# HGRN2 chunk products as eight levels of one form, dilated scores with both row halves in one step

## The chip, the cores and the metric

The kernel runs on one core of one Trainium2 chip. The metric is the device time of one execution in microseconds (us); the median of three runs of the kernel before is 2509.81 us (2506.52 to 2512.93). A core has a matmul engine (TensorE, PE in the profile; its weight loads are PEld), a vector engine (DVE), a scalar engine (ACT), a GpSimd engine (POOL) and a sync engine (SP) that here only issues DMAs. Each works through its own instructions in order; they wait for each other by semaphores. SBUF is the core's working memory with 128 partitions, PSUM the memory that PE writes, in eight banks of 128 x 512 f32.

## The reference

Two layers of a decoder trunk: 512 tokens, width 1024, f32. Each layer has a parallel token mixer of four branches (A dilated sliding-window attention in three groups, B differential attention, C HGRN2, D RWKV-7), gates, a merge, a cross-attention and a gated MLP with a convolution. The change touches C and A. C works in chunks of 64 tokens (4 heads of width 64); for one chunk it computes

```python
b = jnp.cumsum(lfc, axis=2)
diff = b[:, :, :, None, :] - b[:, :, None, :, :]
decay = jnp.exp(jnp.where(causal, diff, -jnp.inf))
att = jnp.einsum('bhtk,bhtsk,bhsk->bhts', qc, decay, kc)
o = o_inter + jnp.einsum('bhts,bhsv->bhtv', att, ic)
```

so that each product of query t and key s carries a decay for each of 64 channels. In A, each of three groups has 4 heads of width 64; a query of a block of 128 sees its own block and, in the first group, the one before:

```python
s = jnp.einsum('brhnqd,brhnkd->brhnqk', qb, kb).astype(F32) * dh ** -0.5
m = jnp.max(s, axis=-1, keepdims=True)
p = jnp.exp(s - m)
```

## The kernel before

**Two kinds of PE work.** The projections are dense: 128x128 weights against 512 tokens, each as three fp32r products of high and low parts (mm3 and ws_run, L405 on). A weight chunk `wst` comes by DMA, ACT casts the high part `whi` (L482), DVE subtracts for the low part `wlo` (L483), and the products gather in one of four PSUM banks (tag `pd`, L422). The branches' own products are small f32 matmuls, of which each is two MATMUL instructions in the trace; they use the other four banks (tag `ps`, L425).

**The order of the work** is set in Python by a planner (Weave, L294). It has one queue of dense work and a number of chains, which are generators. When a chain says `yield v`, its next step falls due at the planner's PE time plus v times a scale (0.856, for the chains `At` 1.84 times that, `csc`); until then dense work is put on PE. PE time is counted by rule (Tensor.matmul, L281: n/600 us for an f32 matmul of n columns), not measured. The tile framework then orders the instructions of each engine and adds the waits.

**Branch C** (branch_c, chain `Cb`) runs on PE while projection D (`Dp`) is the dense work. `b` is the running sum of the log decays. The chunk products are split by dyadic levels: level(h) (L816) makes X, which holds q times exp(b - b_mid) in the later h tokens of each block of 2h and k times exp(b_mid - b) in the earlier h; a product of X with itself is right in the upper right h x h corner of each block, and the mask U{h} takes just that corner. DVE subtracts (L823), ACT takes two exps, POOL makes two products (L826, L827). Levels 16, 8, 4 and 2 (L868 on) take for each row half p (two heads live in partitions 0 to 63, two in 64 to 127) and each pair of token blocks u one bank, four matmuls of 64 rows x 128, then a copy_predicated on DVE (L879) into `catt`. Levels 64 and 32 are there in a form of their own: narrow products for just the corners (L855 on), 64x64 and 32x32, with ACT copies. The diagonal and its neighbour (s = t and s = t - 1) are sums over channels: POOL and DVE make the products `cpr` (L804 to L810), PE sums them by a matrix of two columns, `hsel` (L836 on), ACT copies the sums to `csm`, and DVE spreads them over an identity (L852, L853).

**Dp's evacuation** shares the engines: DVE takes each finished bank to `Dp_draw` (L1030), POOL makes the difference of neighbouring tokens `Dp_ddd` (L1031), DVE mixes them into `dr`, `dk`, ... (L1034).

**Branch A** (attn_a, chain `At`) goes through banks of scores: a_scores puts the products of one row half p into one bank, DVE masks and takes the maxima, ACT the exps; a_turn transposes on PE and copies on ACT; a_out multiplies by v. With two halves there are 8 banks in the first group and 4 in each of the others, and the steps of neighbouring banks overlap. b_scores, in branch B, already takes the two row halves in turn, each into its own bank, and so do the products of D (`Db_ps<-dfar,dfbk`).

**rstd** (L576) sums squares over partitions by matmuls with two columns of ones. With `perm=True` (the chain `r1`, L1940) it also does so for the tokens at stride 4, into four more columns that no line reads except to copy them (L747).

Of the kernel before, what the change touches and what calls it, by code (L numbers as in the profile page):

```python
# [372 lines left out]
class Trunk:  # L373
# [1680 lines left out]
```

## Time and profile before

| | |
|---|---|
| median of three runs | 2509.81 us |
| the profiled execution, its own time | 2507.58 us |
| its span from first to last instruction | 2505.8 us |
| PE busy | 2456.6 us (98%), 13360 instructions |
| DVE busy | 1538.8 us (61%) |
| ACT busy | 996.3 us (40%) |
| POOL busy | 498.4 us (20%) |

The profile is of one execution. PE works nearly all the time, the other engines much less; what PE waits for is short in sum. The matmuls are pipelined, so the busy time of one says little about its cost: the distance between the starts of two neighbours does. A dense matmul of 128x512 starts every 0.227 us at the full granted clock (1.00 in the windows, 2.4 GHz) and every 0.427 us at 0.50 (1.2 GHz).

### The profile page before, as it was taken

Reading aid. Unit: us, or ns where it says so; the run is one execution under the profiler, and the core shown is the slowest. Engines: PE = TensorE matmul, PEld = TensorE weight load, DVE = VectorE, ACT = ScalarE, POOL = GpSimd, SP = SyncE. Lnnn points to the kernel's source line nnn. Section 1 sums busy time; section 2 is a strip of 40 time slices with the busy share of each in tenths; the row PEclk is TensorE's granted clock in tenths of the full one; section 3 lists DMA queues with packets and bytes.
Section 4 is the critical chain, followed back from the end, with each engine's and each line's share of the span. In section 5 each row is a group of like instructions: output and inputs, shape, how many; then the busy total and the mean of one; then the engine's idle time right before and its main releaser. Section 6 shows DMA issues by size and latency. Waiting matters only on the chain.

```text
span 2505.8 us, 34400 instructions
## 1 busy us (share of the span) xinstructions
PE 2456.6 (98%) x13360; PEld 2036.9 (81%) x13360; DVE 1538.8 (61%) x2751; ACT 996.3 (40%) x1769; POOL 498.4 (20%) x382
## 2 busy tenths in 40 slices
PE   8999999999999999999999999999999999999997
PEld 7777888778889888888897788877888898888886
DVE  7678356855655667366466773577556565762763
ACT  6332423434344444234362325244343344441441
POOL 1421033234010111001123110423330101110112
PEclk9899999999999999999999999999999999999998
DMA  4224334223423222322321242332234241222321
GB/s 171 82 87 145 98 116 145 67 66 126 143 97 132 88 93 93 101 93 101 127 88 52 92 146 95 121 119 77 67 123 143 98 152 60 92 101 93 101 93 59
DMA packets 89602, 259.62 MB, mean 104 GB/s; under 512 B 18144, under 2 KB 21856, under 8 KB 89440
## 3 DMA queue, kind: packets, MB, share of 16 engines
q1 hardware_dynamic: 57168, 205.81, 24.7%
q10 hardware_dynamic: 25872, 30.52, 3.7%
q0 software_dynamic: 6400, 21.11, 2.6%
q8 instruction: 105, 1.72, 0.3%
q14 instruction: 57, 0.47, 0.1%
HBM read 234.26 MB, written 23.13 MB: 103 GB/s over the span
## 4 chain that ended last, share of the span: by engine, by line
PE 92%; DVE 5%; ACT 1%; issue 1%; DMA 1%; POOL 0%; DVEq 0%; ACTq 0%; SPq 0%; POOLq 0%
PE ffn_pd L287 29%; PE A_pd L287 7%; PE Bp_pd L287 5%; PE Dp_pd L287 4%; PE Cp_pd L287 4%; PE ga_pd L287 3%; PE mo_pd L287 3%; PE mq_pd L287 3%; PE mix_pd L287 3%; PE gd_pd L287 3%; PE gc_pd L287 3%; PE Db_ps L287 3%; PE Cb_ps L287 3%; PE At_ps L287 2%; PE mk_pd L287 2%; PE mv_pd L287 2%
## 5 line engine op out<-in xcount | busy, mean ns | idle before, releaser
L482 ACT CAST whi<-wst 128x1024 fp32r<-128x1024 f32 x388 | 406.0, 1051 | 743.5 <-PE ffn_pd L287 216.1
L483 DVE TENSOR_TENSOR wlo<-wst,whi 128x1024 fp32r<-128x1024 f32 x388 | 494.1, 1277 | 212.3 <-ACT whi L482 211.0
L287 PE MATMUL ffn_pd<-xgh,whi 128*128 128x512 f32 x704 | 274.3, 390 | 0.0
L287 PE MATMUL ffn_pd<-xgh,wlo 128*128 128x512 f32 x704 | 273.9, 389 | 0.0
L287 PE MATMUL ffn_pd<-xgl,whi 128*128 128x512 f32 x704 | 273.9, 389 | 0.0
L1918 POOL TENSOR_TENSOR ffn_ft<-ffn_ft,ffn_fc 128x512 f32<-128x512 f32 x44 | 60.2, 1368 | 545.6 <-DVE ffn_fu L1904 350.3
L287 PEld LDWEIGHTS ffn_pd<-xgl,whi 128*128 128x128 f32 x704 | 132.1, 188 | 27.5
L287 PEld LDWEIGHTS ffn_pd<-xgh,wlo 128*128 128x128 f32 x704 | 132.1, 188 | 27.5
L287 PEld LDWEIGHTS ffn_pd<-xgh,whi 128*128 128x128 f32 x704 | 132.2, 188 | 27.2
L287 PE MATMUL ffn_pd<-fh,whi 128*128 128x512 f32 x352 | 136.9, 389 | 0.0
L287 PE MATMUL ffn_pd<-fl,whi 128*128 128x512 f32 x352 | 136.9, 389 | 0.0
L287 PE MATMUL ffn_pd<-fh,wlo 128*128 128x512 f32 x352 | 136.9, 389 | 0.0
L287 PE MATMUL A_pd<-xgh,whi 128*128 128x512 f32 x256 | 107.1, 418 | 0.0
L287 PE MATMUL A_pd<-xgh,wlo 128*128 128x512 f32 x256 | 100.9, 394 | 0.0
L287 PE MATMUL A_pd<-xgl,whi 128*128 128x512 f32 x256 | 100.5, 393 | 0.0
L1905 DVE TENSOR_TENSOR ffn_fu<-ffn_pd,r_rbc 128x512 f32<-128x512 f32 x88 | 60.4, 688 | 43.8 <-PE ffn_pd L287 43.5
L1468 POOL TENSOR_TENSOR A_rp<-A_rp,snr 128x512 f32<-128x512 f32 x24 | 52.1, 2172 | 174.4 <-DVE A_rp L1467 174.4
L530 DVE TENSOR_TENSOR fl<-ffn_ft,fh 128x512 fp32r<-128x512 f32 x44 | 30.5, 692 | 90.6 <-ACT fh L529 90.6
L529 ACT CAST fh<-ffn_ft 128x512 fp32r<-128x512 f32 x44 | 27.3, 621 | 144.8 <-POOL ffn_ft L1918 144.8
L574 POOL TENSOR_TENSOR mo_sqa<-mo_sqa,mo_sqt 128x512 f32<-128x512 f32 x14 | 23.6, 1684 | 297.8 <-ACT mo_sqa L570 257.9
L1907 ACT ACTIVATE ffn_fc<-ffn_fu,cvt 128x512 f32<-128x512 f32 x88 | 71.7, 817 | 26.8 <-DVE ffn_fu L1905 26.6
L287 PEld LDWEIGHTS ffn_pd<-fl,whi 128*128 128x128 f32 x352 | 66.1, 188 | 13.8
(601 smaller groups left out, 6342.8 us busy)
## 6 DMA issues: line engine op xcount, KB each, us to landing
wst<-in_wst_dram SPq DMA_DIRECT2D x388, 512.0 KB, 3.5
gb_gate<-gb_gu ACTq DMA_DIRECT2D x16, 256.0 KB, 2.2
gd_gate<-gd_gu ACTq DMA_DIRECT2D x16, 256.0 KB, 2.1
gc_gate<-gc_gu ACTq DMA_DIRECT2D x16, 256.0 KB, 2.0
pc_gu<-gc_gate POOLq DMA_DIRECT2D x16, 256.0 KB, 3.9
pd_gu<-gd_gate POOLq DMA_DIRECT2D x16, 256.0 KB, 3.0
pb_gu<-gb_gate POOLq DMA_DIRECT2D x16, 256.0 KB, 3.5
x<-in_x_dram ACTq DMA_DIRECT2D x13, 256.0 KB, 3.8
```

Source lines behind the costliest of these rows:

```text
L287: return self.te.matmul(out, lhsT, rhs, **kw)
L482: nc.scalar.copy(hi, st)
L483: nc.vector.tensor_sub(lo, st, hi.bitcast(F32))
L529: nc.scalar.copy(dst[0], src)
L530: nc.vector.tensor_sub(dst[1], src, dst[0].bitcast(F32))
L574: (eng or nc.gpsimd).tensor_add(acc[:, :n], acc[:, :n], t[:, :n])
L1468: nc.gpsimd.tensor_mul(t2, t2, self.snr)
L1905: nc.vector.tensor_mul(u[:, 2:514], ps, self.rb)
L1907: nc.scalar.activation(acc, u[:, 2:514], AF.Identity, scale=self.cv('cw2', ch), bias=self.cv('cb', ch))
L1918: nc.gpsimd.tensor_mul(th, th, cc[1])
```

## The change

In C the sums by `hsel` and the narrow form are gone. There are eight levels of one form: 0 (the diagonal: k against q themselves), 1 (made by first(): exp of one step's decay times q in odd tokens, a copy of k in even ones), 64, 32, 16, 8, 4, 2. The four `catt` tiles are set to zero on POOL at the start. A level is one step: for each u two banks, and the four products of the row halves p = 0 and p = 1 in turn, 16 matmuls of 64 rows x 128 in four banks. Levels 64 and 32 are copied by ACT, the others by DVE's copy_predicated (there is a new mask U0). In A, a step takes both row halves: their scores in turn into two banks, then the transposes of both, then the outputs of all four heads in one bank. The first group has 4 steps instead of 8, the others 2 instead of 4, with longer yields. r1 no longer makes the permuted sums. The diff, cut to its core:

```diff
-for _h in (1, 2, 4, 8, 16, 32):
+for _h in (0, 1, 2, 4, 8, 16, 32):
...
+    u[:, UM['U0']:UM['U0'] + 128] = p == f
...
-            if perm:
-                self.te.matmul(ps[:, 2 * (nt + t):2 * (nt + t) + 2], acc[:, t:512:4], self.ones[:, 0:2],
-                                 start=True, stop=True)
+        nw = nt
...
-        pr = [ar.alloc([P, 2, 512], name='cpr') for _ in range(2)]
         od = lambda x, o: x.rearrange("p j (n a) -> p j n a", a=2)[:, :, :, o]
-        nc.gpsimd.tensor_mul(pr[0], q, k)
-        nc.scalar.activation(od(pr[1], 0), od(lf, 1), AF.Exp)
-        nc.vector.tensor_mul(od(pr[1], 0), od(pr[1], 0), od(q, 1))
-        nc.vector.tensor_mul(od(pr[1], 0), od(pr[1], 0), od(k, 0))
-        nc.gpsimd.memset(od(pr[1], 1), 0.0)
-        ar.free(lf)
...
-        X64, X64t = level(64)
-        X32, X32t = level(32)
-        yield 4
-        att = [[None, None], [None, None]]
+        def first():
+
+            X = ar.alloc([P, 2, 512], name='cX')
+            nc.scalar.activation(od(X, 1), od(lf, 1), AF.Exp)
+            nc.gpsimd.tensor_mul(od(X, 1), od(X, 1), od(q, 1))
+            nc.gpsimd.tensor_copy(od(X, 0), od(k, 0))
+            ar.free(lf)
+            return X, X
...
         mm = self.te.matmul
-        ps = self.pss()
-        for x in range(2):
-            for t in range(NT):
-                for j in range(2):
-                    o = 16 * x + 4 * t + 2 * j
-                    mm(ps[:, o:o + 2], pr[x][:, j, t * P:(t + 1) * P], self.c('hsel'), start=True, stop=True)
-        sm = self.small([P, 2, NT, 2, 2], 'csm', 1)
-        nc.scalar.copy(sm.rearrange("p x t j q -> p (x t j q)"), ps[:, 0:32])
-        ar.free(pr)
-        yield 4
...
-            sv = [bc(sm[:, x, 2 * u:2 * u + 2, :, p], 3, P) for x in range(2)]
-            nc.vector.tensor_tensor(av, bc(bc(self.c('ident'), 1, 2), 1, 2), sv[0], op=ALU.mult)
-            nc.vector.copy_predicated(av, bc(bc(self.um_('U1'), 1, 2), 1, 2), sv[1])
-            ps = self.pss().rearrange("p (n t) -> p n t", n=4)
-            for n in range(4):
-                j, o = n % 2, (2 * u + n // 2) * P
-                mm(ps[0:64, n, 64:128], X64[r, j, o:o + 64], X64[r, j, o + 64:o + 128], start=True, stop=True)
-                for c in (0, 64):
-                    mm(ps[c:c + 32, n, c + 32:c + 64], X32[r, j, o + c:o + c + 32],
-                       X32[r, j, o + c + 32:o + c + 64], start=True, stop=True)
-            nc.scalar.copy(a[0:64, :, 64:128], ps[0:64, :, 64:128])
-            for c in (0, 64):
-                nc.scalar.copy(a[c:c + 32, :, c + 32:c + 64], ps[c:c + 32, :, c + 32:c + 64])
-            att[p][u] = a
...
+        att = [[ar.alloc([P, 4, P], name='catt') for u in range(2)] for p in range(2)]
+        for a in att[0] + att[1]:
+            nc.gpsimd.memset(a, 0.0)
+        levels = [0, 1, 64, 32, 16, 8, 4, 2]
+        nxt = ((k, q), None)
+        for n, h2 in enumerate(levels):
+            (lhs, rhs), Xt = nxt
+            if n + 1 < len(levels):
+                X, xt = level(levels[n + 1]) if n else first()
+                nxt = ((X, X), xt)
             yield 3
-            for p, u in idx:
-                r = slice(p * 64, p * 64 + 64)
-                ps = self.pss().rearrange("p (n t) -> p n t", n=4)
-                for n in range(4):
-                    j, o = n % 2, (2 * u + n // 2) * P
-                    mm(ps[:, n], X[r, j, o:o + P], X[r, j, o:o + P], start=True, stop=True)
-                nc.vector.copy_predicated(att[p][u], bc(self.um_('U%d' % h2), 1, 4), ps)
-                yield 0.3
-            ar.free(Xt)
+            for u in range(2):
+                ps = [self.pss().rearrange("p (n t) -> p n t", n=4) for _ in range(2)]
+                for x in range(4):
+                    j, o = x % 2, (2 * u + x // 2) * P
+                    for p in range(2):
+                        r = slice(p * 64, p * 64 + 64)
+                        mm(ps[p][:, x], lhs[r, j, o:o + P], rhs[r, j, o:o + P], start=True, stop=True)
+                for p in range(2):
+                    a = att[p][u]
+                    if h2 >= 32:
+                        for c in range(0, P, 2 * h2):
+                            nc.scalar.copy(a[c:c + h2, :, c + h2:c + 2 * h2],
+                                           ps[p][c:c + h2, :, c + h2:c + 2 * h2])
+                    else:
+                        nc.vector.copy_predicated(a, bc(self.um_('U%d' % h2), 1, 4), ps[p])
+            if Xt is not None:
+                ar.free(Xt)
...
-        rr = slice(p * 64, p * 64 + 64)
...
+        pv = [self.pss()[:, :nn * w].rearrange("p (n k) -> p n k", n=nn) for _ in range(2)]
         for n in range(nn):
             t, j = ts_[n // 2], n % 2
-            self.te.matmul(pv[:, n], q[rr, j, t * P:(t + 1) * P], k[rr, j, (t + 1 - nb) * P:(t + 1) * P],
-                           start=True, stop=True)
+            for p in range(2):
+                rr = slice(p * 64, p * 64 + 64)
+                self.te.matmul(pv[p][:, n], q[rr, j, t * P:(t + 1) * P],
+                               k[rr, j, (t + 1 - nb) * P:(t + 1) * P], start=True, stop=True)
...
+    def a_turn(self, ss, nn, w):
+        for s in ss:
+            pt = self.pss()
+            sf = s.rearrange("p n k -> p (n k)")
+            for n in range(nn * w // P):
+                self.te.transpose(pt[:, n * P:(n + 1) * P], sf[:, n * P:(n + 1) * P], self.c('ident'))
+            self.nc.scalar.copy(sf, pt[:, :nn * w])
...
-        banks = [(p, ts_, 1) for ts_ in ((0, 1), (2, 3)) for p in range(2)] if g else \
-            [(p, (t,), 2 if t else 1) for t in range(NT) for p in range(2)]
-        po = {}
+        banks = [((0, 1), 1), ((2, 3), 1)] if g else [((t,), 2 if t else 1) for t in range(NT)]
         s1 = self.a_scores(g, q, k, st, *banks[0])
         v = v()
-        yield 4
+        yield 6
         for x in range(len(banks)):
             nxt = self.a_scores(g, q, k, st, *banks[x + 1]) if x + 1 < len(banks) else None
             yield 0
             s = self.a_turn(*s1)
-            yield 1.3
-            self.a_out(v, o, po, s, *banks[x])
-            yield 1
+            yield 1.8
+            self.a_out(v, o, s, *banks[x])
+            yield 2
...
-        chain('r1', lambda: self.rstd(self.acc, perm=True), 'go', delay=self.lat_sq)
+        chain('r1', lambda: self.rstd(self.acc), 'go', delay=self.lat_sq)```

**Order on PE, layer 1, where C's levels begin (the kernel after).** `Cb_ps_11085` and `Cb_ps_11086` are the first two banks of level 0, `Cb_ps_11130` the first of level 1, `cX_11053` what first() made, `Dp_pd` the dense work.

```order
L288 MATMUL Dp_pd_11075<-xgh_10109,wlo_11079 128x512
L288 MATMUL Cb_ps_11085<-cq_10543,ck_10973 128x128
L288 MATMUL Cb_ps_11086<-cq_10543,ck_10973 128x128
...
L288 MATMUL Cb_ps_11098<-cq_10543,ck_10973 128x128
L288 MATMUL Dp_pd_11075<-xgh_10110,whi_11078 128x512
...
L288 MATMUL Dp_pd_11075<-xgl_10120,whi_11078 128x512
L288 MATMUL Dp_pd_11075<-xgh_10118,wlo_11079 128x512
L288 MATMUL Cb_ps_11130<-cX_11053 128x128
L288 MATMUL Cb_ps_11131<-cX_11053 128x128
```

Level 0 takes all four banks of tag `ps` (11085, 11086, 11097, 11098), and level 1 follows 15 dense matmuls later; each of the other levels stands 15 dense matmuls behind the one before it as well. Level 0 stands where the `hsel` sums stood, three dense matmuls earlier.

**Order on DVE, layer 1.** Before, ahead of and at the first work on `catt`:

```order
L1034 SCALAR_TENSOR_TENSOR dr_10988<-Dp_ddd_11043,cvt_10544,Dp_draw_11042 128x512
L1030 TENSOR_TENSOR Dp_draw_11106<-Dp_pd_11048,r_rbc_10692 128x512
L483 TENSOR_TENSOR wlo_11382<-wst_11379,whi_11381 128x1024
L1034 SCALAR_TENSOR_TENSOR dr_10988<-Dp_ddd_11107,cvt_10544,Dp_draw_11106 128x512
L852 TENSOR_TENSOR catt_11162<-cst,Cb_csm_11142 128x512
```

After, the same place (L1012 and L1008 are L1034 and L1030 of before):

```order
L1012 SCALAR_TENSOR_TENSOR dr_10958<-Dp_ddd_11013,cvt_10518,Dp_draw_11012 128x512
L1008 TENSOR_TENSOR Dp_draw_11069<-Dp_pd_11018,r_rbc_10662 128x512
L484 TENSOR_TENSOR wlo_11344<-wst_11341,whi_11343 128x1024
L1012 SCALAR_TENSOR_TENSOR dr_10958<-Dp_ddd_11070,cvt_10518,Dp_draw_11069 128x512
L857 COPY_PREDICATED catt_11045<-um,Cb_ps_11085 128x512
L857 COPY_PREDICATED catt_11047<-um,Cb_ps_11086 128x512
...
L857 COPY_PREDICATED catt_11045<-um,Cb_ps_11130 128x512
```

The copies that empty level 0's banks stand where the spreading over the identity stood, behind two `dr`, each of which reads a `Dp_ddd` of POOL.

**Order on POOL, layer 1.** Before, from the last products of X ahead of the first `Dp_ddd`:

```order
L826 TENSOR_TENSOR cX_11327<-cX_11327,cq_10569 128x128x4
L827 TENSOR_TENSOR cX_11327<-cX_11327,ck_11003 128x128x4
L1031 TENSOR_TENSOR Dp_ddd_11043<-Dp_draw_11042 128x512
L1031 TENSOR_TENSOR Dp_ddd_11107<-Dp_draw_11106 128x512
L1031 TENSOR_TENSOR Dp_ddd_11251<-Dp_draw_11250 128x512
L826 TENSOR_TENSOR cX_11397<-cX_11397,cq_10569 128x256x2
```

After:

```order
L816 TENSOR_TENSOR cX_11319<-cX_11319,cq_10543 128x128x4
L817 TENSOR_TENSOR cX_11319<-cX_11319,ck_10973 128x128x4
L816 TENSOR_TENSOR cX_11377<-cX_11377,cq_10543 128x256x2
L817 TENSOR_TENSOR cX_11377<-cX_11377,ck_10973 128x256x2
L1009 TENSOR_TENSOR Dp_ddd_11013<-Dp_draw_11012 128x512
L1009 TENSOR_TENSOR Dp_ddd_11070<-Dp_draw_11069 128x512
```

The two products of level 2 (tiles of 128x256x2), which stood behind the third `Dp_ddd`, now stand ahead of the first. Ahead of all these POOL had one product `cpr` of 128x1024 and now has first()'s copy and product of 128x512 each. Layer 0 has the same order at these places.

## Rows read from the trace of the kernel before

**Rows 1.** Chain that ended last: share of the span by engine.

```profile
PE 92%; DVE 5%; ACT 1%; issue 1%; DMA 1%; POOL 0%; DVEq 0%; ACTq 0%; SPq 0%; POOLq 0%
```

**Rows 2.** PE's waits: line, releaser, us in total, times, longest.

```profile
PE Bb_ps L291 <- DVE bp L1550: 14.9, 13, 1.9
...
PE Cb_ps L291 <- DVE cy L947: 1.0, 2, 0.5
```

**Rows 3.** PE in time: start, us, line, out<-in, count; hsel, layer 0.

```profile
75.56 4.29 PE L287 MATMUL Cb_ps<-cst,cpr 128*128 128x2 f32 x32
79.72 0.77 PE L287 MATMUL Dp_pd<-xgh,whi 128*128 128x512 f32 x1
...
85.30 0.39 PE L287 MATMUL Dp_pd<-xgl,whi 128*128 128x512 f32 x1
```

**Rows 4.** PE in time, the narrow products of levels 64 and 32, layer 0.

```profile
86.55 7.75 PE L287 MATMUL Cb_ps<-cX 64*64 64x64 f32 x96
94.23 0.79 PE L287 MATMUL Dp_pd<-xgh,whi 128*128 128x512 f32 x1
...
98.97 0.39 PE L287 MATMUL Dp_pd<-xgh,wlo 128*128 128x512 f32 x1
```

**Rows 5.** PE in time, one of 16 blocks of levels 16 to 2.

```profile
99.67 0.39 PE L287 MATMUL Dp_pd<-xgh,wlo 128*128 128x512 f32 x1
99.98 1.16 PE L287 MATMUL Cb_ps<-cX 64*128 64x128 f32 x8
101.07 0.50 PE L287 MATMUL Dp_pd<-xgh,whi 128*128 128x512 f32 x1
101.41 0.40 PE L287 MATMUL Dp_pd<-xgl,whi 128*128 128x512 f32 x1
```

**Rows 6.** PE in time, branch B's scores with the row halves in turn.

```profile
405.41 0.71 PE L287 MATMUL Bb_ps<-bk,bq 64*128 64x128 f32 x8
406.06 0.50 PE L287 MATMUL pc_pd<-yTh,whi 128*128 128x512 f32 x1
...
412.44 1.14 PE L287 MATMUL Bb_ps<-bk,bq 64*128 64x256 f32 x8
```

**Rows 7.** PE in time, one of 6 score blocks of A's first group.

```profile
513.61 1.13 PE L287 MATMUL At_ps<-ak,aq 64*128 64x256 f32 x4
```

**Rows 8.** PE in time, sums of squares: r1 in layer 1, and another without perm.

```profile
734.09 0.95 PE L287 MATMUL r_ps<-ones,mix_sqa 128*128 128x2 f32 x8
...
1256.73 2.80 PE L287 MATMUL r_ps<-ones,ffn_sqa 128*128 128x2 f32 x16
1259.39 0.77 PE L287 MATMUL Cp_pd<-xgh,whi 128*128 128x512 f32 x1
...
1262.87 0.40 PE L287 MATMUL Cp_pd<-xgh,wlo 128*128 128x512 f32 x1
```

**Rows 9.** POOL in time, up to the first Dp_ddd, layer 0.

```profile
72.66 2.37 POOL L827 TENSOR_TENSOR cX<-cX,ck 128x512 f32<-128x512 f32 x1
...
78.65 1.27 POOL L827 TENSOR_TENSOR cX<-cX,ck 128x512 f32<-128x512 f32 x1
79.87 1.04 POOL L1031 TENSOR_TENSOR Dp_ddd<-Dp_draw 128x512 f32<-128x512 f32 x1
```

**Rows 10.** DVE in time, the work on catt, both layers.

```profile
86.53 1.28 DVE L852 TENSOR_TENSOR catt<-cst,Cb_csm 128x512 f32<-128x512 f32 x2
...
101.25 0.74 DVE L879 COPY_PREDICATED catt<-um,Cb_ps 128x512 f32<-128x512 uint8 x1 [3.47 <-PE Cb_ps L287]
...
1327.02 1.29 DVE L852 TENSOR_TENSOR catt<-cst,Cb_csm 128x512 f32<-128x512 f32 x2
```

**Rows 11.** PE in time, layer 1: where the hsel sums start.

```profile
1311.57 4.64 PE L287 MATMUL Cb_ps<-cst,cpr 128*128 128x2 f32 x32
```

**Rows 12.** Stretches: length, busy and count of PE, PEld, DVE, ACT, POOL; PEclk, DMA, GB/s.

```profile
78.40:85.10 6.70, 6.70 (x21) 5.54 (x21) 3.83 (x6) 1.13 (x2) 3.93 (x4) 0.50 0.10 39
...
208.70:213.60 4.90, 4.75 (x65) 4.19 (x64) 4.68 (x9) 0.00 (x0) 3.61 (x5) 1.00 0.53 158
```

More of the change, by code (lines that the diff above doesn't have):

```diff
@@ L574, in sq_acc, with rstd @@
             (eng or nc.gpsimd).tensor_add(acc[:, :n], acc[:, :n], t[:, :n])
-    def rstd(self, acc, n=512, perm=False, keep=True):
+    def rstd(self, acc, n=512, keep=True):
         nc = self.nc
@@ L580, in rstd @@
         ps = self.pss()
-        cols = self.small([P, 8], 'rcol', 2)
-        v = self.small([P, 8], 'rvar', 2)
-        nw = 2 * nt if perm else nt
+        cols = self.small([P, 4], 'rcol', 2)
+        v = self.small([P, 4], 'rvar', 2)
         for t in range(nt):
@@ L730, in proj_c @@
         self.open(l, 'C')
-        hcol = self.small([P, 8], 'hcol', 2)
+        hcol = self.small([P, 4], 'hcol', 2)
         q = ar.alloc([P, 2, 512], name='cq')
@@ L1640, in a_scores @@
         mask = self.c('mA2') if g == 2 else self.c('mA0')[:, (2 - nb) * P:]
-        s = ar.alloc([P, nn, w], name='as')
-        nm = self.small([P, 4], 'anm', 3)
-        mx = self.small([P, 4], 'amx', 3)
-        nc.vector.tensor_tensor(s, pv, bc(mask, 1, nn), op=ALU.add)
-        nc.vector.tensor_reduce(mx[:, :nn], s, axis=AX.X, op=ALU.max)
-        nc.vector.tensor_scalar(nm[:, :nn], mx[:, :nn], -sc, None, op0=ALU.mult)
-        for n in range(nn):
-            t, h = ts_[n // 2], 2 * (n % 2) + p
-            nc.vector.tensor_copy(st[:, t, h:h + 1], mx[:, n:n + 1])
-            nc.scalar.activation(s[:, n], s[:, n], AF.Exp, scale=sc, bias=nm[:, n:n + 1],
-                                 accum_out=st[:, t, 4 + h:5 + h])
@@ L1652, in a_scores @@
-        return s, nn, w
-    def a_turn(self, s, nn, w):
-        pt = self.pss()
-        sf = s.rearrange("p n k -> p (n k)")
-        for n in range(nn * w // P):
-            self.te.transpose(pt[:, n * P:(n + 1) * P], sf[:, n * P:(n + 1) * P], self.c('ident'))
-        self.nc.scalar.copy(sf, pt[:, :nn * w])
-        return s
-    def a_out(self, v, o, po, s, p, ts_, nb):
-        nc, ar = self.nc, self.ar
-        for n in range(2 * len(ts_)):
-            t, h = ts_[n // 2], 2 * (n % 2) + p
-            if t not in po:
-                po[t] = self.pss()
-            for b in range(nb):
-                kb = t + 1 - nb + b
-                self.te.matmul(po[t][:, h * 64:h * 64 + 64], s[:, n, b * P:(b + 1) * P],
-                               v[:, kb, h * 64:h * 64 + 64], start=b == 0, stop=b == nb - 1)
-        ar.free(s)
-        if p == 1:
-            for t in ts_:
-                nc.scalar.copy(o[:, t], po.pop(t)[:, 0:256])
+        nm = self.small([P, 2, 4], 'anm', 2)
@@ new lines, in a_scores @@
+        mx = self.small([P, 2, 4], 'amx', 2)
+        ss = []
+        for p in range(2):
+            s = ar.alloc([P, nn, w], name='as')
+            nc.vector.tensor_tensor(s, pv[p], bc(mask, 1, nn), op=ALU.add)
+            nc.vector.tensor_reduce(mx[:, p, :nn], s, axis=AX.X, op=ALU.max)
+            ss.append(s)
+        nc.vector.tensor_scalar(nm[:, :, :nn], mx[:, :, :nn], -sc, None, op0=ALU.mult)
+        for p in range(2):
+            for n in range(nn):
+                t, h = ts_[n // 2], 2 * (n % 2) + p
+                nc.vector.tensor_copy(st[:, t, h:h + 1], mx[:, p, n:n + 1])
+                nc.scalar.activation(ss[p][:, n], ss[p][:, n], AF.Exp, scale=sc, bias=nm[:, p, n:n + 1],
+                                     accum_out=st[:, t, 4 + h:5 + h])
@@ new lines, in a_scores, with a_out @@
+        return ss, nn, w
+    def a_turn(self, ss, nn, w):
[5 more added lines that the diff above has]
+            self.nc.scalar.copy(sf, pt[:, :nn * w])
+        return ss
+    def a_out(self, v, o, ss, ts_, nb):
+        nc, ar = self.nc, self.ar
+        po = self.pss().rearrange("p (t f) -> p t f", t=2)
+        for x, t in enumerate(ts_):
+            for h in range(4):
+                for b in range(nb):
+                    kb = t + 1 - nb + b
+                    self.te.matmul(po[:, x, h * 64:h * 64 + 64],
+                                   ss[h % 2][:, 2 * x + h // 2, b * P:(b + 1) * P],
+                                   v[:, kb, h * 64:h * 64 + 64], start=b == 0, stop=b == nb - 1)
+        ar.free(ss)
+        nc.scalar.copy(o[:, ts_[0]:ts_[-1] + 1], po[:, :len(ts_)])
@@ L1938, in chain @@
             w.chain(n(name), gen, N(*need), delay)
-        chain('r1', lambda: self.rstd(self.acc, perm=True), 'go', delay=self.lat_sq)
+        chain('r1', lambda: self.rstd(self.acc), 'go', delay=self.lat_sq)
         add('Cp', lambda: self.proj_c(l, xg(), n('r1')), 'go')
```

18 lines of the change are left out of this document (1 added, 17 removed).

## The prediction

> **What bounds the kernel now.** I read the chain that ended last first: 92% of it is PE [rows 1]. Then PE's waits: the longest sum, branch B's, is 14.9 us, and C's products wait 1.0 us in all; A's are not in the list [rows 2]. So a microsecond less of PE work is a microsecond of the result, and a new wait of PE costs its full length. Then I read PE in time, block by block, by the distance between starts: a dense matmul starts 0.23 us after its neighbour at the full clock and 0.43 at half, and what a small block takes beyond that is its cost. A block of eight MATMULs of 64 rows x 128 on one row half holds PE from 99.98 to 101.07, 1.09 us, and 0.08 us of entry and 0.11 of re-entry lie around it: 1.28 us [rows 5]. The same eight with the halves in turn take from 405.41 to 406.06, 0.65 us [rows 6]. I read this as turns of the array: eight turns against four, (1.09 - 0.65) / 4 = 0.11 us each, and 0.21 at the start. At 256 columns eight in turn take 1.14 us [rows 6], as long as four on one half, 1.13 [rows 7]: the two halves run fully beside each other.
>
> **The change in C, on PE.** Removed, per layer: the sums by hsel, 79.72 - 75.56 = 4.16 us, and behind them 13 dense spacings that take 85.30 - 79.72 = 5.58 us instead of 13 x 0.227 = 2.95, so 2.63 more [rows 3]; the granted clock there is 0.50, 1.2 GHz [rows 12]. The narrow products of levels 64 and 32: 94.23 - 86.55 = 7.68 and 0.1 of entry, and 4.74 for 11 spacings of 2.50, so 2.24 [rows 4]. The 16 blocks of levels 16 to 2: 16 x 1.28 = 20.5 [rows 5]. Sum 37.3 us. Added: eight levels. One is 32 MATMULs, 16 turns with the halves beside each other: 0.65 + 12 x 0.11 = 1.99, with entry and re-entry 2.2 [rows 5, 6]; eight are 17.5. Gain 19.8 a layer, 39.6 for both.
>
> **A, on PE.** Only the scores change their price; transposes and outputs stay as many. In groups two and three eight blocks of eight MATMULs at 1.28 (the same shape) [rows 5] become four of sixteen in turn, 8 turns, 1.28: 5.1 less; where transposes follow without re-entry a little less, I take 4.7. In the first group six blocks of four at 256 columns become three of eight of the same length, 3 x (1.13 + 0.1) = 3.7 [rows 6, 7]; its two small first blocks become one, about 1.0. Sum 9.4 a layer, 18.8. The exps of twice as many scores now stand between scores and transposes, but 30 dense matmuls (6.8 us) and an output block lie there as cover, and no wait of A is in the list before, so I add none.
>
> **r1.** 2.80 us becomes 0.95, as the sum without perm has it: 1.85 a layer, 3.7. In layer 1 the eight spacings behind it take 1262.87 - 1259.39 = 3.48 instead of 1.82, less the usual re-entry 1.55 [rows 8]; I count that as gone. Sum 5.2. All gains: 39.6 + 18.8 + 5.2 = 63.6 us.
>
> **The wait that comes.** A level takes all four `ps` banks, so level 1 can't start before DVE has emptied level 0's. The order puts these copies behind two `dr`, which need two `Dp_ddd` of POOL, and POOL now has two more products of X ahead of them: at 1.27 us [rows 9] 2.5 us later. The memsets on POOL stand far ahead and cost nothing; the rest of DVE's queue there is as before, so I move its work on `catt` from 86.53 and 1327.02 [rows 10] to 89.0 and 1329.6, and the first bank is free 0.74 us later [rows 10], at 89.8 and 1330.3. PE is there sooner. Layer 0: level 0 starts three dense matmuls before 75.56 [rows 3], at 75.0, takes 2.0, and 15 dense with entries 3.5: 80.5. Layer 1: from 1311.57 [rows 11] the same way 1316.5. The waits are 9.3 and 13.8 us. Before, hsel's bank alone was taken there, and nothing had to be emptied by DVE, so this wait was not seen. What is queued behind it on PE is all dense work, so nothing hides it; DVE and POOL go on. The third and fourth bank come free two copies later, so level 1 stretches by about 1.0 each. Behind a wait of this length I expect the half clock that follows the hsel sums: there 2.63, behind the narrow form 2.24 [rows 3, 4]; part falls into the wait, I take 1.5 each. Sum 23.1 + 2.0 + 3.0 = 28.1. Below: copies no later than `catt` before, 86.53 and 1327.02 plus 0.74, and no clock loss: 6.8 + 11.3 = 18. Above: the two products and first()'s copy at 2.37 us each, as where DVE is in their way [rows 9], 7.1 instead of 2.5 later, and full clock losses: 13.9 + 18.4 + 7 = 39.
> The Trainium skill, "TensorEngine Tiling (Array Packing)", section "Gotcha 1: PSUM Pressure", says that different row tiles write to different PSUM banks and so raise the pressure on PSUM. The trace shows no such wait before (1.0 us in all); without one the sum would be 2444, with it 2472.
>
> **The sum.** The profiled execution took 2507.6 us, its span 2505.8; 2507.6 - 63.6 + 28.1 = 2472.1. The median of the runs is 2.2 above that execution, so I predict 2474. By the bounds of the wait alone: 2464 to 2485.
>
> **Rivals.**
> First, no wait worth the name: POOL or DVE come to `Dp_ddd` and the copies sooner, because the `cpr` products are gone from both (one of 128x1024 on POOL, two on DVE). For it: POOL works a fifth of the time in the mean. Against it: the order, where the copies stand behind both `dr`. Time: 2509.8 - 63.6 = 2446, with half the wait 2460.
> Second, DVE becomes the bound at every level: between two levels it has four copies, 4 x 0.74 = 3.0 us, and Dp's own work for 15 of a bank's 24 dense matmuls, an estimate of 1.9 us from the same 0.74 (two instructions of 128x512 and a `wlo` of twice the size, 3.0 x 15/24), and the branch's other products; against that PE's period is 2.2 + 15 x 0.227 = 5.6 us. That is close; one to two us on each of five levels and both layers give 10 to 20: 2484 to 2494. Levels 64 and 32, emptied by ACT, would be spared.
> The Trainium skill states this too (same page, section "PSUM Bottleneck"): tiling speeds up the matmuls, not the evacuation, which may become the bottleneck. The copy's 0.74 us agrees so far as the copies fill over half of the period.
> Third, slower: in C and A the halves do not run beside each other, say because in C weights and moving data come from the same tile X. Then a level is 32 turns, 32 x 0.11 + 0.4 = 3.9, C gains 37.3 - 31.4 = 5.9 a layer, A nothing, and 2509.8 - 11.8 - 5.2 + 28.1 = 2521. It turns the sign where a level takes over (37.3 - (28.1 - 5.2) / 2) / 8 = 3.2 us and A gains nothing. Against it: two branches show the pairs, B here [rows 6] and D, whose 64 MATMULs fill 4.9 us, gaps between banks among them [rows 12], where 64 turns alone would be 7.
> Fourth, slower too: eight levels of 64 rows, 45 us of C, at half clock. That costs 15 x 0.2 = 3 us a level, 48 in all: about 2522. Against it: D's stretch of 64-row products, 208.7 to 213.6, ran at 1.00 (2.4 GHz); the stretch at 0.50 followed the two-column products [rows 12].
>
> **How the numbers follow.** Forecast 0.62, less wait 0.14, DVE as the bound 0.16, halves not beside each other 0.03, clock 0.02, and 0.03 that gains are lost elsewhere to within the noise. A measurement of this kernel tells 0.3%, 7.5 us, from no change. Faster 0.91 (the first three, a little of the third being lost), same 0.04, slower 0.05. The range from 2452 to 2494 leaves out most of the case with no wait at all (0.10), the slower ones (0.05) and a tail of DVE (0.03).
>
> **What would show it.** In the changed trace a level of C should hold PE about 2.0 us, with starts in pairs; between levels 0 and 1 PE should wait some 9 and 14 us for a copy_predicated, with `Dp_ddd` on POOL starting about 2.5 us after the place it has now; the other levels should follow each other after 15 dense matmuls; the granted clock should be 0.50 near that wait and no longer behind r1. In A a step's scores should take as long as one half's did. The prediction is wrong if level 1 finds its banks free, if levels 16 to 2 each wait for DVE, or if a level takes 3 us or more.

## The result and the profile after

The changed kernel takes 2476.0 us (median of 4 runs, 2472.6 to 2478.2) where the kernel before took 2508.2 in the same comparison: a ratio of 0.987, with an interval from 0.985 to 0.989. The forecast was 2474. The profiled execution has a span of 2474.5 us, so 31.3 of its 2505.8 are gone.

The page of the changed kernel (busy time, share of the span, instructions; then the chain that ended last):

```profile
PE 2405.6 (97%) x13344; PEld 2005.7 (81%) x13344; DVE 1528.1 (62%) x2731; ACT 991.9 (40%) x1759; POOL 504.7 (20%) x390
...
PE 87%; DVE 6%; POOL 2%; ACT 2%; issue 1%; DMA 1%; DVEq 0%; ACTq 0%; SPq 0%; POOLq 0%
```

PE's share of the chain fell from 92% [rows 1] to 87%, and POOL, at 0% before, has 2%: something that PE waits for now leads back to POOL. PE's waits (line, releaser, us in total, times, longest) name it:

```profile
PE Cb_ps L288 <- DVE catt L857: 14.5, 2, 8.8
...
PE Dp_pd L288 <- DVE wlo L484: 3.7, 1, 3.7
```

Both are new: the list of the kernel before has neither. The two waits for `catt` lie between levels 0 and 1 of branch C, one in each layer; the one for `wlo` lies just ahead of level 0 in layer 1. PE in layer 0 (start, us, line, out<-in, count, idle before and its releaser):

```profile
72.83 0.39 PE L288 MATMUL Dp_pd<-xgh,wlo 128*128 128x512 f32 x1
73.15 2.06 PE L288 MATMUL Cb_ps<-cq,ck 64*128 64x128 f32 x32
75.14 0.50 PE L288 MATMUL Dp_pd<-xgh,whi 128*128 128x512 f32 x1
...
87.68 4.39 PE L288 MATMUL Cb_ps<-cX 64*128 64x128 f32 x32 [8.85 <-DVE catt L857]
92.00 0.63 PE L288 MATMUL Dp_pd<-xgh,whi 128*128 128x512 f32 x1
...
95.46 0.39 PE L288 MATMUL Dp_pd<-xgh,wlo 128*128 128x512 f32 x1
...
101.39 2.06 PE L288 MATMUL Cb_ps<-cX 64*128 64x128 f32 x32
...
107.01 2.06 PE L288 MATMUL Cb_ps<-cX 64*128 64x128 f32 x32
```

Level 0 holds PE from 73.15 to 75.14, 1.99 us for its 32 MATMULs. They start in pairs, one on each row half, 6 or 7 ns apart, and a pair follows the other after 105 ns. After 15 dense matmuls PE stands still for 8.85 us, and level 1 takes 4.32 instead of 1.99. A later level starts 107.01 - 101.39 = 5.62 us after its neighbour, without a wait. The wait ends with DVE, whose queue there reads (same columns)

```profile
84.00 1.22 DVE L484 TENSOR_TENSOR wlo<-wst,whi 128x1024 fp32r<-128x1024 f32 x1
...
86.15 0.75 DVE L1012 SCALAR_TENSOR_TENSOR dr<-Dp_ddd,cvt,Dp_draw 128x512 f32<-128x512 f32 x1 [0.93 <-POOL Dp_ddd L1009]
86.82 1.32 DVE L857 COPY_PREDICATED catt<-um,Cb_ps 128x512 f32<-128x512 uint8 x2
```

and DVE's `dr` waits for POOL:

```profile
79.15 1.48 POOL L817 TENSOR_TENSOR cX<-cX,ck 128x512 f32<-128x512 f32 x1
80.59 1.03 POOL L1009 TENSOR_TENSOR Dp_ddd<-Dp_draw 128x512 f32<-128x512 f32 x1
84.16 1.96 POOL L1009 TENSOR_TENSOR Dp_ddd<-Dp_draw 128x512 f32<-128x512 f32 x1 [2.53 <-DVE Dp_draw L1007]
```

The chain is as forecast: X products, two `Dp_ddd`, two `dr`, the first copy at 86.82 and PE at 87.68. Now layer 1, PE, then DVE, then POOL:

```profile
1294.45 0.80 PE L288 MATMUL Dp_pd<-xgh,wlo 128*128 128x512 f32 x1 [3.71 <-DVE wlo L484]
1295.17 3.79 PE L288 MATMUL Cb_ps<-cq,ck 64*128 64x128 f32 x32
1298.89 0.79 PE L288 MATMUL Dp_pd<-xgh,whi 128*128 128x512 f32 x1
...
1309.06 4.29 PE L288 MATMUL Cb_ps<-cX 64*128 64x128 f32 x32 [5.66 <-DVE catt L857]
```

```profile
1292.10 4.49 DVE L484 TENSOR_TENSOR wlo<-wst,whi 128x1024 fp32r<-128x1024 f32 x2
...
1308.19 2.53 DVE L857 COPY_PREDICATED catt<-um,Cb_ps 128x512 f32<-128x512 uint8 x4
```

```profile
1291.06 2.25 POOL L816 TENSOR_TENSOR cX<-cX,cq 128x512 f32<-128x512 f32 x1
```

Here the waiting falls into two pieces, 3.71 us for a weight part `wlo` ahead of level 0 and 5.66 for the copies. The kernel before had the same two `wlo` ahead of its `hsel` sums, but there it was POOL that was late (before; DVE, then POOL):

```profile
1305.98 2.35 DVE L483 TENSOR_TENSOR wlo<-wst,whi 128x1024 fp32r<-128x1024 f32 x2
...
1300.65 9.18 POOL L826 TENSOR_TENSOR cX<-cX,cq 128x512 f32<-128x512 f32 x1 [3.37 <-ACT cX L824]
```

Before, DVE did two `wlo` in 2.35 us, and a product of POOL lasted 9.18 beside DVE's work; after, the two `wlo` take 4.49 and POOL's products about 2.25 each (times on POOL are rough). Why the two engines share the time differently is not shown. The clock in these stretches (columns as in [rows 12]):

```profile
87.70:92.00 4.30, 4.30 (x32) 4.01 (x32) 4.30 (x8) 0.00 (x0) 0.00 (x0) 0.50 0.07 27
92.50:100.00 7.50, 7.50 (x57) 6.14 (x56) 5.76 (x6) 5.40 (x8) 3.34 (x2) 1.00 0.23 72
...
1295.00:1300.00 5.00, 5.00 (x36) 4.41 (x36) 5.00 (x5) 1.05 (x1) 5.00 (x4) 0.50 0.66 211
1239.50:1250.00 10.50, 10.50 (x56) 8.95 (x55) 4.31 (x28) 3.46 (x7) 0.00 (x0) 1.00 0.00 1
```

After these waits PE ran at 0.50 (1.2 GHz), busy all the time: level 1 of layer 0 from 87.7 to 92.0, and in layer 1 the stretch from 1295 to 1300. From 92.5 on it is 1.00 again, and behind the shortened r1 it is 1.00 throughout. In A and r1 (PE):

```profile
492.23 0.68 PE L288 MATMUL At_ps<-ak,aq 64*128 64x128 f32 x4
492.84 0.49 PE L288 MATMUL A_pd<-xgl,whi 128*128 128x512 f32 x1
493.26 0.71 PE L288 MATMUL At_ps<-ak,aq 64*128 64x128 f32 x4
...
503.91 1.13 PE L288 MATMUL At_ps<-ak,aq 64*128 64x256 f32 x8
...
1240.04 0.95 PE L288 MATMUL r_ps<-ones,ffn_sqa 128*128 128x2 f32 x8
```

Eight products of 256 columns take the 1.13 us that four took [rows 7], and r1 the 0.95 of [rows 8]. A's first two small blocks did not become one: a dense matmul still stands between them.

### The profile page after: what moved, and what is told of

Read it like the earlier page. It is cut to its first block, busy times and chain, and to the rows that moved or that the text cites. A ratio compares the mean times of both kernels' runs of the same rounds, so it can differ in the third digit from the quotient of the medians.

```text
span 2474.5 us, 34381 instructions
## 1 busy us (share of the span) xinstructions
PE 2405.6 (97%) x13344; PEld 2005.7 (81%) x13344; DVE 1528.1 (62%) x2731; ACT 991.9 (40%) x1759; POOL 504.7 (20%) x390
## 4 chain that ended last, share of the span: by engine, by line
PE 87%; DVE 6%; POOL 2%; ACT 2%; issue 1%; DMA 1%; DVEq 0%; ACTq 0%; SPq 0%; POOLq 0%
PE ffn_pd L288 29%; PE A_pd L288 7%; PE Bp_pd L288 5%; PE mo_pd L288 4%; PE mq_pd L288 4%; PE mix_pd L288 4%; PE ga_pd L288 4%; PE gd_pd L288 4%; PE gc_pd L288 3%; PE Db_ps L288 3%; PE Dp_pd L288 2%; PE gb_pd L288 2%; PE mv_pd L288 2%; PE mk_pd L288 2%; PE matt_ps L288 2%; PE Cb_ps L288 2%
## 5 line engine op out<-in xcount | busy, mean ns | idle before, releaser
L483 ACT CAST whi<-wst 128x1024 fp32r<-128x1024 f32 x388 | 406.1, 1051 | 786.2 <-PE ffn_pd L288 216.1
L484 DVE TENSOR_TENSOR wlo<-wst,whi 128x1024 fp32r<-128x1024 f32 x388 | 494.4, 1278 | 213.1 <-ACT whi L483 211.9
L288 PE MATMUL ffn_pd<-xgh,whi 128*128 128x512 f32 x704 | 274.3, 390 | 0.0
L288 PE MATMUL ffn_pd<-xgh,wlo 128*128 128x512 f32 x704 | 273.9, 389 | 0.0
L288 PE MATMUL ffn_pd<-xgl,whi 128*128 128x512 f32 x704 | 273.9, 389 | 0.0
L288 PEld LDWEIGHTS ffn_pd<-xgh,wlo 128*128 128x128 f32 x704 | 132.2, 188 | 27.7
L288 PEld LDWEIGHTS ffn_pd<-xgl,whi 128*128 128x128 f32 x704 | 132.2, 188 | 27.3
L288 PEld LDWEIGHTS ffn_pd<-xgh,whi 128*128 128x128 f32 x704 | 132.2, 188 | 27.1
L288 PE MATMUL ffn_pd<-fh,whi 128*128 128x512 f32 x352 | 136.9, 389 | 0.0
L288 PE MATMUL ffn_pd<-fl,whi 128*128 128x512 f32 x352 | 136.9, 389 | 0.0
L288 PE MATMUL ffn_pd<-fh,wlo 128*128 128x512 f32 x352 | 136.9, 389 | 0.0
L288 PE MATMUL A_pd<-xgh,whi 128*128 128x512 f32 x256 | 106.0, 414 | 0.0
L288 PE MATMUL A_pd<-xgh,wlo 128*128 128x512 f32 x256 | 101.2, 395 | 0.0
L288 PE MATMUL A_pd<-xgl,whi 128*128 128x512 f32 x256 | 100.8, 394 | 0.0
L1886 ACT ACTIVATE ffn_fc<-ffn_fu,cvt 128x512 f32<-128x512 f32 x88 | 71.7, 817 | 26.9 <-DVE ffn_fu L1884 26.7
L288 PEld LDWEIGHTS ffn_pd<-fl,whi 128*128 128x128 f32 x352 | 66.1, 188 | 13.8
```

The source lines that it names most:

```text
L288: return self.te.matmul(out, lhsT, rhs, **kw)
L483: nc.scalar.copy(hi, st)
L484: nc.vector.tensor_sub(lo, st, hi.bitcast(F32))
L1886: nc.scalar.activation(acc, u[:, 2:514], AF.Identity, scale=self.cv('cw2', ch), bias=self.cv('cb', ch))
```

## The experiments

**One part alone, and a surprise.** The first pair ran C's part and A's part each alone on the kernel before.

```diff
 # c_only: the edits of the masks and of branch_c only
-for _h in (1, 2, 4, 8, 16, 32):
+for _h in (0, 1, 2, 4, 8, 16, 32):
+        levels = [0, 1, 64, 32, 16, 8, 4, 2]
 # a_only: the edits of a_scores to attn_a only
-    def a_scores(self, g, q, k, st, p, ts_, nb):
+    def a_scores(self, g, q, k, st, ts_, nb):
```

> The kernel before with C's part of the change alone. Theory (on PE C's products gain 39.6 us, and a wait of level 1 for DVE's copies of level 0, with the slow clock around it, gives about 26 back): 13 us less than before, 2495 us (2490 to 2500), and PE's list of waits shows Cb_ps waiting for catt twice, some 9 and 6 us. Rival 1 (the wait eats all of C's gain, and A alone makes the difference): 2508. Rival 2 (C and A each hide part of the other's cost, so that the parts do not add up): under 2488.

> The kernel before with A's part of the change alone. Theory (row halves beside each other halve the price of A's scores, nothing waits): 17 us less than before, 2491 us (2487 to 2495), no wait of At_ps over 1 us in PE's list. Rival (the exps of both halves come too late for the transposes, or the branch that follows waits): 2498 or more.

Measured: 2534.1 us (1.010, 1.009 to 1.012) and 2532.2 (1.009, 1.007 to 1.010). Each part alone makes the kernel slower, both together faster. The blocks themselves were as in the changed kernel, and so were the waits: c_only waits 14.4 us for `catt`, in two, and no wait of `At_ps` is in a_only's list. What differed was the pace of the dense matmuls over the whole program: in the feed-forward network 233.0 and 233.4 ns from start to start in the mean instead of 226.8. None of the edits touch that network. There it shows as fewer PE instructions in a stretch of 100 us (length, PE busy and count, PEclk, DMA, GB/s). With C alone:

```profile
2250.00:2350.00 100.00, 100.00 (x432) 1.00 0.30 94
```

and in the changed kernel:

```profile
2250.00:2350.00 100.00, 100.00 (x443) 1.00 0.29 95
```

The granted clock is 1.00 and the DMA load alike, so neither is the cause. Left was where the tiles lie. By the addresses that the build assigns, the distance in a partition from the weight tiles to the activation tiles is 67840 bytes before and 67584 after, both multiples of 256; with C alone it is 67712 (128 over such a multiple) and with A alone 67776 (64 short of one). So a small tile allocated between them, `cel`, was lengthened, and nothing else:

```diff
-        el = self.small([P, 8], 'cel', 1)
+        el = self.small([P, 40], 'cel', 1)[:, 0:8]   # c_pad, after_pad: 128 bytes more
+        el = self.small([P, 24], 'cel', 1)[:, 0:8]   # a_pad: 64 bytes more
+        el = self.small([P, 16], 'cel', 1)[:, 0:8]   # pad32: 32 bytes more
```

> c_only with one small tile (cel) 128 bytes per partition longer, nothing read from the added part, every engine's order the same. In c_only every dense matmul starts 0.233 us after its neighbour instead of 0.227, over the whole program; the distance in SBUF from the weight tiles (whi) to the activation tiles (xgh) is 67840 bytes before, 67584 after, both multiples of 256, and 67712 in c_only, which is not. Theory (this distance, not the order, is what slows c_only): the distance is 67840 here, dense spacing 0.227 and 2495 us (2490 to 2500), 39 us less than c_only. Rival (the slower spacing comes with C's part alone, by its instructions or their number): 2534 again.

> a_only with the same small tile 64 bytes longer, orders the same. The distance is 67776 bytes in a_only (64 short of a multiple of 256) and 67840 here. Theory (distance): dense spacing 0.227, 2491 us (2487 to 2496), 41 us less than a_only. Rival (A's part alone slows the dense work): 2532 again.

> The changed kernel with the small tile 128 bytes longer, orders the same; the distance becomes 67712 bytes as in c_only. Theory (distance): dense spacing 0.233 over the whole program, some 40 us more than the changed kernel: 2515 us (2508 to 2520), slower than the kernel before. Rival (only the programs with one part of the change are slow, whatever their addresses): 2476 again, spacing 0.227.

> The changed kernel with the small tile 32 bytes longer: distance from weight to activation tiles 67616 bytes, 32 more than a multiple of 256. Where the distance was 128 bytes or 64 short of such a multiple, dense matmuls started 0.233 us apart, at multiples 0.227. Theory (any distance that is not a multiple of 256 is slow): spacing 0.233, 2513 us (2508 to 2518). Rival (only distances that are multiples of 64 but not of 256 are slow, or this one is better than a multiple): spacing 0.227 or less, 2476 or less.

Measured: c_pad 2499.1 us (0.996, 0.995 to 0.997), a_pad 2489.9 (0.992, 0.990 to 0.993), after_pad 2513.3 (1.0015, 1.0006 to 1.0024), pad32 2517.9 (one run), each inside the range that its theory gave. The padding takes the slowness away from either part and brings it to the whole change. C alone, padded (the stretch as above):

```profile
2250.00:2350.00 100.00, 100.00 (x443) 1.00 0.31 100
```

The whole change, padded:

```profile
2250.00:2350.00 100.00, 100.00 (x432) 1.00 0.30 95
```

The four kernels whose distance is a multiple of 256 bytes (67840 three times, 67584) ran at 226.8 ns, the four others (67712 twice, 67776, 67616) at about 233; the three pairs with and without padding differ by 35 to 43 us a program (differences of the ratios, times 2508). What is shown is that shifting the tiles behind `cel` against those ahead of it does this. Neither side's own address does: the first activation tile lies at 113952 in the kernel before, which is fast, and in c_only and after_pad, which are slow, and the first weight tile `whi` at 46240 in c_only, slow, and in c_pad, fast. That it is the distance between weights and activations, rather than another pair on the two sides, is inferred.

With equal placement the parts add up within the noise: C -9.5 us, A -20.6 (ratios times 2508, each give or take 3), the whole -33.1 (give or take 5). The 3.0 left are less than that noise; r1 was not run alone, and the trace gives it 5.0 of starts (below).

**The halves one after the other.** In a level, all four products of p = 0, then those of p = 1:

```diff
-                for x in range(4):
-                    j, o = x % 2, (2 * u + x // 2) * P
-                    for p in range(2):
+                for p in range(2):
+                    for x in range(4):
+                        j, o = x % 2, (2 * u + x // 2) * P
```

> The changed kernel with the products of a level in C ordered by half (all of p = 0 of a pair of token blocks, then all of p = 1), the same products, banks and copies. Theory (the gain in C is that neighbouring products on different row halves run beside each other): a level holds PE 3.7 to 3.9 us instead of 2.0, 16 levels, of which the two level 0 fall partly into the wait behind them: 24 us more than the changed kernel, 2500 us (2495 to 2503). Rival (the gain is fewer blocks and the narrow forms gone, the pairs bring nothing): 2476, levels of 2.0 us.

Measured: 2486.2 us (0.991, 0.989 to 0.992), 10 us over the changed kernel where 24 were expected. A level (PE):

```profile
105.87 2.82 PE L288 MATMUL Cb_ps<-cX 64*128 64x128 f32 x32
108.61 0.50 PE L288 MATMUL Dp_pd<-xgh,whi 128*128 128x512 f32 x1
```

It holds PE 2.74 us, between 1.99 in turn and the 3.9 of the third rival's 32 turns. The turn order is worth 0.75 us a level, so the third rival is false, and its price was too high as well: a run of four products (eight MATMULs) on one half already overlaps the other half's in part, for MATMULs on one half start 0.11 us apart, which makes 3.5 us for 32.

**Where level 1's wait comes from.** Two runs only reorder the levels, to put other work between levels 0 and 1 or to leave them for the end:

```diff
-        levels = [0, 1, 64, 32, 16, 8, 4, 2]
+        levels = [64, 32, 0, 1, 16, 8, 4, 2]   # lead64
+        levels = [64, 32, 16, 8, 4, 2, 1, 0]   # last0
+        # X comes from first() at level 1, from level(h) at the others, wherever it stands
```

> The changed kernel with the levels in the order 64, 32, 0, 1, 16, 8, 4, 2, so that the two levels that ACT copies come first and DVE's first copies are due two levels later. Theory (the wait is that DVE reaches level 0's copies only behind the dr that need POOL's chain; nothing else holds level 1): the waits of 8.8 and 5.7 us of Cb_ps for catt fall under 2 us each, the slow clock behind them goes, 15 to 22 us less than the changed kernel: 2456 us (2453 to 2462). Rival 1 (DVE is the bound over all levels, the wait comes back at a later level): 2470 to 2476. Rival 2 (ACT's copies come late, so that level 32 or 0 waits for ACT): a wait of Cb_ps for ACT's catt of over 3 us, 2465 or more.

> The changed kernel with the levels in the order 64, 32, 16, 8, 4, 2, 1, 0. In the order 64, 32, 0, 1, 16, ... the wait had moved to ACT: the copies of level 32 stood behind an exp for level 2, whose subtraction on DVE stood behind both dr. Here all subtractions come before the dr, and the exp ahead of level 32's copies needs no DVE. Theory (each wait is a copy queued behind something that needs POOL's chain): in layer 1 no wait of Cb_ps over 1 us, in layer 0 one of some 3 us stays (ACT is late there by a DMA issue that waits for DVE); 2457 us (2453 to 2462). Rival (DVE's copies of six levels in a row become the bound): levels 8 to 0 wait 1 us or more each for DVE, 2466 or more.

Measured: 2463.5 us (0.982, 0.980 to 0.983) and 2467.3 (0.983, 0.982 to 0.985): 12 and 9 us better than the change; both theories' ranges (2453 to 2462) were missed. In lead64 the wait moved to ACT's copies (PE's waits):

```profile
PE Cb_ps L288 <- ACT catt L860: 5.7, 2, 3.3
...
PE Cb_ps L288 <- DVE catt L863: 1.2, 1, 1.2
```

and ACT shows why: level 32's copies (L860) stand behind the exps of a later level (L814), which wait for a DVE subtraction that stands behind both `dr`:

```profile
85.39 1.28 ACT L814 ACT_TABLE_LOAD   x1 [3.14 <-DVE cX L813]
86.69 0.69 ACT L814 ACTIVATE cX<-cX 128x512 f32<-128x512 f32 x1
...
87.82 2.15 ACT L860 COPY catt<-Cb_ps 32x128 f32<-32x128 f32 x8
```

In last0 it is split between both engines, ACT in layer 0 and DVE in layer 1:

```profile
PE Cb_ps L288 <- DVE catt L863: 5.6, 1, 5.6
PE Cb_ps L288 <- ACT catt L860: 4.6, 1, 4.6
```

So each of the three orders tried has a copy that comes late. The next two take POOL out of the way of the first `dr`:

```diff
-            nc.gpsimd.tensor_sub(dd, raw[:, 0:512], raw[:, 1:513])
+            (nc.vector if n < 2 else nc.gpsimd).tensor_sub(dd, raw[:, 0:512], raw[:, 1:513])   # ddd2
+            (nc.vector if n < 3 else nc.gpsimd).tensor_sub(dd, raw[:, 0:512], raw[:, 1:513])   # lead_ddd3, on lead64
```

> The changed kernel with the difference Dp_ddd of the first two tiles of projection D (those of dr) on DVE instead of POOL; levels in the order 0, 1, 64, ..., DVE's order otherwise the same, level 0's copies still behind both dr. Theory (level 1 waits for level 0's copies, these for dr, and dr for POOL, which comes to Dp_ddd only after its products of X): PE's waits of 8.8 and 5.7 us for catt fall under 1 us each, the half clock behind them goes, DVE's two subtractions a layer cost PE nothing; 2457 us (2453 to 2463). Rival 1 (DVE itself is late there, because POOL's products hold its two-input instructions up): waits of over 3 us for catt stay, 2466 or more. Rival 2 (level 1 waits for something else, as X of level 1): 2474.

> The order 64, 32, 0, 1, 16, 8, 4, 2 with the first three Dp_ddd (dr, dr, dk) on DVE. Theory (both waits of the order with 64 and 32 first come from POOL's chain, by way of dr or of the subtraction for level 2 behind it): no wait of Cb_ps for ACT or DVE over 1.5 us in either layer, 2453 us (2449 to 2460), some 3 us less than with the levels in the changed kernel's order, since DVE's first copies are due later. Rival (ACT is late by its own queue): a wait for ACT's catt of 3 us or more in layer 0 stays, 2458 or more.

Measured: 2470.0 us (0.985, 0.983 to 0.986) and 2459.5 (0.981, 0.979 to 0.982). ddd2 leaves 9.5 of the 14.5 us of waiting for `catt`: its theory failed, and its first rival came true. DVE, and POOL behind it, show what stood in for POOL's delay:

```profile
78.75 1.05 DVE L1009 TENSOR_TENSOR Dp_ddd<-Dp_draw 128x512 f32<-128x512 f32 x1
79.72 2.28 DVE L484 TENSOR_TENSOR wlo<-wst,whi 128x1024 fp32r<-128x1024 f32 x1
81.93 1.97 DVE L1012 SCALAR_TENSOR_TENSOR dr<-Dp_ddd,cvt,Dp_draw 128x512 f32<-128x512 f32 x1
...
79.22 1.71 POOL L817 TENSOR_TENSOR cX<-cX,ck 128x512 f32<-128x512 f32 x1
80.89 2.46 POOL L816 TENSOR_TENSOR cX<-cX,cq 128x512 f32<-128x512 f32 x1
```

While POOL still works on X, `wlo` takes 2.28 us and `dr` 1.97. In the changed kernel `dr` takes 0.75 with POOL idle, and `wlo`, which starts at 84.00 ahead of POOL's `Dp_ddd` at 84.16, takes 1.22; there it is `Dp_ddd` that lasts 1.96 instead of 1.03. Each time the instruction that starts later is the one that lasts longer than it does elsewhere. lead_ddd3 still waits for `catt`, 3.6 us for ACT's copies and 1.0 for DVE's, where its theory allowed 1.5 at a time and 2.5 came. So the last run moved the cause itself, the X products of levels 64 to 2, to DVE, and left the rest of the change as it is:

```diff
-            nc.gpsimd.tensor_mul(   # both products of level()
+            nc.vector.tensor_mul(
```

> The changed kernel with the two products of each X (levels 64 to 2) on DVE instead of POOL, 12 instructions a layer; Dp_ddd stays on POOL, levels in the order 0, 1, 64, .... With Dp_ddd on DVE the waits for catt had only fallen from 14.5 to 9.5 us, and DVE's instructions with two SBUF inputs took 1.7 to 2.5 us there instead of 0.7 to 1.2, while POOL worked on X. Theory (half of the wait is POOL's chain ahead of Dp_ddd, the other half that the products of X on POOL hold up DVE): both go; DVE does 12 products of about 0.68 us but its own work there is fast again; waits for catt under 1 us in layer 0, the wait for wlo of 3.7 us in layer 1 under 1 us as well: 2453 us (2449 to 2460). Rival (DVE is simply full there, so that 8 us more of work on it make its copies later): the waits for catt stay over 9 us in sum, 2470 or more.

Measured: 2458.7 us (2458.0 to 2461.6; 0.981, 0.979 to 0.982). PE's wait:

```profile
PE Cb_ps L288 <- DVE catt L857: 6.2, 3, 3.6
```

and DVE:

```profile
74.17 0.69 DVE L816 TENSOR_TENSOR cX<-cX,cq 128x512 f32<-128x512 f32 x1
...
77.05 1.22 DVE L484 TENSOR_TENSOR wlo<-wst,whi 128x1024 fp32r<-128x1024 f32 x1
...
79.20 0.75 DVE L1012 SCALAR_TENSOR_TENSOR dr<-Dp_ddd,cvt,Dp_draw 128x512 f32<-128x512 f32 x1 [0.94 <-POOL Dp_ddd L1009]
79.87 2.54 DVE L857 COPY_PREDICATED catt<-um,Cb_ps 128x512 f32<-128x512 uint8 x4
```

A product costs DVE 0.69 us where POOL took 1.26 to 2.49; `dr` and `wlo` are back at 0.75 and 1.22, the copies start at 79.87 instead of 86.82, and the wait for `wlo` is gone. This is the fastest kernel of the study, level with lead_ddd3, 17 us under the change and 49 under the kernel before; 12 of the 17 are the waits themselves (14.5 + 3.7 less 6.2). Of the 6.2 us that remain 1.3 lie in layer 0, where under 1 was forecast, and 4.8 in layer 1, where DVE has four products of X, a subtraction and a `wlo` between the two `dr`: there the rival, a full DVE, holds in part. Both kernels' edits together were not run, nor was a way found to lose these 6.2.

## Why the prediction was right, and where it was not

The prediction's main steps held: the price of a level, the wait between levels 0 and 1 and its cause in layer 0. The figures of this part are sums of the distances between neighbouring starts on PE, by the output of the first of the two, in the profiled executions before and after.

- C, gain and wait together: 11.5 us forecast, 13.6 measured (`Cb` -21.5, `Dp` +7.9). The level's price was right, 1.99 against 2.0, and so were the starts in pairs. (0.65 + 12 x 0.11 is 1.97, not 1.99, and C's products waited 1.5 us before, not 1.0: 0.5 for `Cb_cbd` were passed over. Neither moves the forecast.)
- The wait and the clock: 28.1 us forecast. From the dense matmul ahead of level 0 to the one 15 behind level 1, layer 0 took 95.46 - 72.83 = 22.63 us; two levels and 30 dense matmuls without a wait are 2 x 5.6 = 11.2, so 11.4 were lost (forecast 9.3 + 1.0 + 1.5 = 11.8). Layer 1 lost 1317.02 - 1290.57 - 11.2 = 15.25 in the same way, counted from where the dense matmul ahead of level 0 was due (forecast 16.3). Sum 26.7. Of the extras, half clock was the larger part: level 1 of layer 0 takes 2.33 us more than 1.99 with its clock at 0.50 all through, so little is left for the third and fourth bank, to which the forecast gave 1.0 a layer.
- In layer 0 the forecast put both ends of the wait some 2 us too late, so that the wait itself, 8.85 against 9.3, hardly changed: r1, at 25.9, is 1.85 us shorter in this layer too, so the whole of D came sooner, a shift that the forecast did not carry on to 75.0 and 86.53. POOL's first `Dp_ddd` started at 80.59 instead of 79.87 [rows 9], which against a layer that comes 1.85 sooner is 2.6 later; 2.5 were forecast.
- Layer 1's division was wrong: 13.8 forecast for `catt`, 5.66 measured, plus 3.71 for `wlo` and two levels at half clock, 3.72 and 4.22 between starts instead of 1.99. The failed step is "the rest of DVE's queue there is as before". Its order was as before, its times were not: the two `wlo` beside POOL's work took 4.49 us together where they had taken 2.35, and PE waited for the first of them. The 13.8 for `catt` was 8.1 too much, and what the forecast did not have, the wait for `wlo` and a level 0 at half clock, came to 3.7 + 1.7, with dense matmuls at half clock besides. That came out nearly even; the sum was right partly by this luck.
- A: 18.8 forecast, 16.9 measured (`At` -13.2, the dense work around it and `pb`, `ga` -3.8). The missing two are the "about 1.0" a layer for the first two blocks, which stay split.
- r1: 5.2 forecast, 5.0 measured (-3.7 for the sums, -1.3 for the dense work behind them).
- Elsewhere 4.4 us were added in small pieces (D's and B's blocks about 3.2 of them), not forecast. C's part alone, padded, adds 3.9 outside `Cb` and `Dp` in the same way, so much of it seems to come with that part. Total -31.1.
- Rivals. No wait: false for the change, but x_dve and lead_ddd3, with 6.2 and 4.6 us of waiting for `catt` left, came to 2458.7 and 2459.5, near the 2460 that it named for half the wait: most of the wait hangs on POOL's products. DVE the bound at every level: false, levels follow each other after 15 dense matmuls. Halves not beside each other: false. Half clock throughout: false; among the levels 0.50 stands only near the waits.
- What the prediction didn't see was a fifth case: had the change moved the tiles to a distance that is no multiple of 256 bytes, as each of its parts does, it would have been 2513 as in after_pad, no gain. That the forecast of 2474 came out hung on this accident of allocation, which no row of the profile before shows. That was luck.

## What to carry to other kernels

Where a block takes all buffers at once, price the engine that empties them by its queue, not by its instruction; and when the wait is behind a slow helper engine, try moving that engine's products as well as reordering the consumers: here the first gained 17 us, while the second gained 9 to 12 and moved part of the wait to another engine. Before a small edit is judged, compare the pace of work that it doesn't touch: if that has changed at the same granted clock, look at where the tiles lie, and read the edit's own worth with a padded placement.

## What the runs showed of the hardware

- The pace of dense matmuls depended on placement: 226.8 ns apart or about 233, at a granted clock of 1.00 in both, some 35 to 43 us a program.
- MATMULs of 64 rows on the two row halves ran beside each other in turn (a level 1.99 us), and in part even in runs of eight on one half (2.74 us).
- DVE instructions with two inputs in SBUF took 1.97 instead of 0.75 us (`dr`) and 2.28 instead of 1.22 (`wlo`) beside POOL's products. The Trainium skill, "SBUF — State Buffer", section "Who interferes with whom", says that a DVE instruction with two SBUF inputs contends with a GpSimd instruction that reads SBUF, and that the order of issue decides which of the two is blocked. The trace agrees: the one that started later lasted longer in the pairs of ddd2 and of the changed kernel shown above, and POOL's products took 1.26 to 2.49 us for the same shape.
